# Moving every float32r operand of TensorE to a 256-byte boundary in SBUF by padding the pools

## The chip, the cores and the metric

The kernel runs on one core of one Trainium2 chip. The metric is device time in microseconds of one execution; smaller is better. The time before is the median of three runs. A separate execution was taken with the hardware profiler, and all rows below come from it.

## The reference

One layer of a hybrid encoder, applied to a prompt of 1024 tokens and a sample of 256 tokens that share all weights; model width 1024, feed-forward width 2816, four heads everywhere.

```python
def encoder_layer(x, mem, ...):
    proj = rmsnorm(x, norm_mix_w) @ w_in
    qkv_raw, ab, dn_gate, sg_u, sg_v, gate_a, gate_b = jnp.split(proj, ...)
    y_a = deltanet_branch(qkv_raw, ab, dn_gate, ...) @ w_up_a
    y_b = spatial_gating_branch(sg_u, sg_v, ...) @ w_up_b
    x = x + (sigmoid(gate_a) * y_a + sigmoid(gate_b) * y_b) @ w_out
    x = x + memory_cross_attention(rmsnorm(x, norm_xa_w), rmsnorm(mem, norm_mem_w), ...)
    gu = rmsnorm(x, norm_ffn_w) @ ffn_w_gate_up
    return x + (silu(gu[..., :D_FF]) * gu[..., D_FF:]) @ ffn_w_down
```

`deltanet_branch` is a bidirectional gated delta rule in chunks. A final RMSNorm follows. All inputs and outputs are float32.

## The kernel before

Activations lie feature-major: 128 features on the partitions, tokens along the free dimension, in the three blocks of `BLOCKS` (512, 512 and 256 tokens). Each large product is done in three TensorE products: an operand x is split into a rounded part hi, of type float32r, and the rest lo = x - hi (`split`, L124 to L126: one ScalarE copy, one subtraction on VectorE or GpSimd), and `mm3` (L110) adds hi·hi, hi·lo and lo·hi into the same PSUM bank. The built program has 6288 float32r matmuls whose moving operand is 512 columns wide, 3888 with 256 columns and 480 with 264 columns (`sgv`, L571). The rest are float32 products: the delta rule's 128-column ones, norms and transposes. A float32 matmul shows as two records in the trace.

The stages stand one behind the other: projections and spatial gating, the delta rule beside the gate projections, memory keys and values, the two up-projections, the output projection (`Seven`, L1281, products with seven instead of eight block multiplications), attention, the gate and up matrices of the feed-forward block (`ff_up`, L2082, from about 1250 us to 1895 us), and its down matrix (`down_prompt`, `down_sample`). Work beside TensorE's main stream (norms, weight splits, the delta rule) is put into the program's order by generators that a clock of TensorE's planned work wakes (`pump`, L71); once built, each engine's order is fixed.

What this case is about is where tiles lie. SBUF tiles come from pools (`pool`, L170). Pools of the default side are stacked upward from the low end of each partition, in the order in which they are opened; pools with `side="right"` are stacked downward from the high end, 229376 bytes. A tile's address so follows from the sizes of all that was opened before it. The first pool, `const` (L175), holds five tiles whose sizes do not add up to a multiple of 256 bytes; behind it follow `w` (weights: `raw`, `whi`, `wlo`), `h` (activations: `hi0`, `lo0`, `hi1` ...) and all later pools of that side. What lies between float32r tiles behind it adds up to multiples of 256 bytes, except where the table below names another offset, so one offset runs through most of the kernel. The addresses of float32r operands, modulo 256 bytes, are:

| operands | byte offset modulo 256 |
|---|---|
| `whi`, `wlo`, `hi*`, `lo*`, `xf`, `bhl`, `yb`, `mhi`, `mlo`, `yhi`, `ylo`, `kv`, `pt` and nearly all else | 96 |
| on the right side, pool `wx` of `Seven` (`ah`, `al`, `r..`), `attq` (`q0`, `q1`), `ffd` (`ahl`) | 224 |
| on the right side, pool `ffn` inside `x2`, `x0` (`t4h`, `t4l`) | 160 |
| `svh`, `svl` as moving operand: 264 columns are 1056 bytes, so the eight slices of a tile start at all multiples of 32 | 0, 32, ... 224 |

By matmul: of the 6288 with 512 columns, 5580 have both operands at 96, 456 have the stationary one at 224 and the moving one at 96, and 252 (those on `t4h`, `t4l`) have the moving one at 160 and the stationary one at 96. Of the 3888 with 256 columns, 3504 are at 96 and 96, and 384 at 96 and 224. Nowhere are both operands at a multiple of 256.

When `sg` is open (its tiles `ab`, `vg`, `wk5`, `gm` and others), the default side reaches to byte 229344: 32 bytes are free.

`decays` (L521) computes the delta rule's decays in five slices z, s_, q_, p_, r_ of the tile `wk5`, each [128, 10, 8], and writes the result into a tile `gm` of [128, 2, 40], 320 bytes (L553 to L557), from which two small TensorE products read it (L562). `s_` is last read at L549, before `gm` is written.

Of the kernel before, what the change touches and what calls it, by code (L numbers as in the profile page):

```python
# [8 lines left out]
F32 = mybir.dt.float32  # L9
# [8 lines left out]
P = 128  # L18
# [36 lines left out]
class Trunk:  # L55
# [44 lines left out]
    def mm(self, out, l, r, start=True, stop=True, more=False):  # L100
        n = 1
        for x in out.shape[1:]:
            n *= x
        if l.dtype == F32R:
            self.clock += max(n, 16) / 2.4 * (1 if n >= 256 else 4)
        else:
            self.clock += (4 * n / 2.4) if n > 1 else 2
        self.nc.tensor.matmul(out, l, r, start=start, stop=stop, skip_group_check=more)  # L108
# [10 lines left out]
    def tr(self, out, x, ident):  # L119
        self.clock += 64  # L120
        self.nc.tensor.transpose(out, x, ident)  # L121
# [42 lines left out]
def trunk_kernel(ctx: ExitStack, tc: tile.TileContext, a):  # L164
# [5 lines left out]
    def pool(name, bufs=1, **kw):  # L170
        if kw.get("space") != DRAM:
            kw["reuse_waits"] = "tile"
        return tc.tile_pool(name=name, bufs=bufs, **kw)

    cp = ctx.enter_context(pool("const"))  # L175
    wp = K.wp = ctx.enter_context(pool("w", 2))
    hp = ctx.enter_context(pool("h"))
    pm = ctx.enter_context(pool("pm", 4, space=PSUM))
# [39 lines left out]
    def bank(p=pq, tag="b"):  # L218
        return p.tile([P, 512], F32, tag=tag, name="bank")
# [195 lines left out]
    r = xp.tile([P, 512], F32, tag="nacc", name="seed", bufs=2)[:, :NS]  # L415
# [73 lines left out]
    sp = ses.enter_context(pool("sg"))  # L489
# [31 lines left out]
    def decays():  # L521
        S.activation(rows[:, 0:8], rows[:, 0:8], AF.Exp)
        wk5 = sp.tile([P, 5, NCH, 8], F32, name="wk5")
        z, s_, q_, p_, r_ = (wk5[:, i] for i in range(5))
        gm = sp.tile([P, 2, 40], F32, name="gm")

        def cols(dst, d):
            return (
                (dst[:, d, 0:32].rearrange("p (h c) -> p c h", h=4), slice(0, 8)),
                (dst[:, d, 32:40].rearrange("p (h c) -> p c h", h=4), slice(8, 10)),  # L530
            )

        S.activation(z, ab[:, :, 0:8], AF.Tanh, scale=0.5)
        for d in range(2):
            for dst, cc in cols(beta, d):
                V.tensor_scalar(out=dst, in0=z[:, cc, 4 * d : 4 * d + 4], scalar1=0.5, scalar2=0.5, op0=ALU.mult, op1=ALU.add)
        V.tensor_tensor(out=r_, in0=ab[:, :, 8:16], in1=rows[:, 8:16].unsqueeze(1).to_broadcast([P, NCH, 8]), op=ALU.add)
        V.scalar_tensor_tensor(out=z, in0=r_, scalar=-1.0, in1=r_, op0=ALU.mult, op1=ALU.max)
        S.activation(z, z, AF.Exp, scale=-1.0)
        yield 1500  # L540

        V.tensor_scalar(out=s_, in0=z, scalar1=2.0, scalar2=None, op0=ALU.add)
        V.reciprocal(s_, s_)
        V.tensor_tensor(out=s_, in0=s_, in1=z, op=ALU.mult)
        V.tensor_tensor(out=q_, in0=s_, in1=s_, op=ALU.mult)
        V.tensor_scalar(out=p_, in0=q_, scalar1=1.0 / 17, scalar2=None, op0=ALU.mult)
        for j in (15, 13, 11, 9, 7, 5, 3):
            V.scalar_tensor_tensor(out=p_, in0=p_, scalar=1.0 / j, in1=q_, op0=ALU.add, op1=ALU.mult)
        V.scalar_tensor_tensor(out=p_, in0=p_, scalar=1.0, in1=s_, op0=ALU.add, op1=ALU.mult)  # L549
        V.tensor_scalar(out=r_, in0=r_, scalar1=0.0, scalar2=None, op0=ALU.max)  # L550
        V.scalar_tensor_tensor(out=p_, in0=p_, scalar=2.0, in1=r_, op0=ALU.mult, op1=ALU.add)
        for d in range(2):
            for dst, cc in cols(gm, d):  # L553
                n = cc.stop - cc.start
                V.scalar_tensor_tensor(
                    out=dst, in0=p_[:, cc, 4 * d : 4 * d + 4], scalar=-1.0,
                    in1=rows[:, 4 * d : 4 * d + 4].unsqueeze(1).to_broadcast([P, n, 4]), op0=ALU.mult, op1=ALU.mult)  # L557
        gr = sp.tile([40, 2, P], F32, name="gr")
        yield 9000
        pr = bank()  # L560
        for d in range(2):
            mm(pr[:40, d * P : (d + 1) * P], gm[:, d, :], tri[d])  # L562
        V.tensor_copy(gr, pr[:40, : 2 * P].rearrange("p (d t) -> p d t", d=2))
        SY.dma_start(grd.rearrange("d r t -> r d t"), gr)
        yield 3000
        pt = bank()
        for d in range(2):
            tr(pt[:, d * 40 : (d + 1) * 40], gr[:, d, :], ident[:40, :40])
        V.tensor_copy(gcol.rearrange("p d r -> p (d r)"), pt[:, :80])
# [79 lines left out]
    for b in (2, 0, 1):  # L649
        K.main(sgv(b))  # L650
        if b == 2:
            bias()
        elif b == 1:
            K.side(decays())
        K.main(sgu(0, b))
        K.main(sgu(1, b))
# [430 lines left out]
    for job in plan:  # L1087
        if job[0] == "conv":
            kind, h = job[1:]
# [290 lines left out]
                evac(x, ps)  # L1380

    wxs = ExitStack()
    so = Seven(a["w_out"], wxs.enter_context(pool("wx", side="right")), mt, smp_h)

    def both_of(*phs):
# [345 lines left out]
    gsd = dp.tile([NFF, P, NS], F32, name="gsd")  # L1731
    x2s, x0s, xhs = ExitStack(), ExitStack(), ExitStack()
    x2p = x2s.enter_context(pool("x2", side="right"))
    x0p = x0s.enter_context(pool("x0", side="right"))
    xhp = xhs.enter_context(pool("xh", side="right"))

# [401 lines left out]
    x2p = ctx.enter_context(pool("x2"))  # L2138
# [336 lines left out]
```

## Time and profile before

| | |
|---|---|
| time, median of three runs | 2192.83 us (2191.4 to 2193.04) |
| span of the profiled execution | 2190.4 us, 2.4 us below that median |
| matmul records | 12436 |
| VectorE busy | 1355.2 us (62%) |
| ScalarE busy | 880.0 us (40%) |
| GpSimd busy | 571.7 us (26%) |
| DMA | 255.13 MB, mean 116 GB/s |

The span is the time from the first to the last instruction of the program; the 2.4 us are what lies around it. On TensorE the length of a record is not what a matmul costs: records overlap, since the next one starts while the last one drains. The cost of one matmul in a stream is the distance from its start to the start of the next, and the timeline view gives the starts.

### The profile page before, as it was taken

To read this page: it belongs to the slowest core of one execution; us is meant where nothing else is said; L and a number is where in the kernel's file an instruction comes from. 1 tells how busy PE (TensorE), PEld (TensorE's weight loads), DVE (VectorE), ACT (ScalarE), POOL (GpSimd) and SP (SyncE) were. 2 spreads that over 40 slices of the span, in tenths; PEclk is the share of its full clock that TensorE was granted. 3 is DMA by queue.
4 is the path that set the end of the run, shared out by engine and by line. 5 is a ranking of instruction groups with operands and counts; after the bars stand their busy time and mean duration, and the time that the engine had idled before them with its cause. 6 is when DMAs were issued, how large, how long until landed. Compare 5 with 4: busy or idle time off the path is not lost.

```text
span 2190.4 us, 32379 instructions
## 1 busy us (share of the span) xinstructions
PE 2175.7 (99%) x12436; PEld 1904.7 (87%) x12436; DVE 1355.2 (62%) x2614; ACT 880.0 (40%) x1649; POOL 571.7 (26%) x379
## 2 busy tenths in 40 slices
PE   9999999999999999999999999999999999999998
PEld 8988888898888899888988888888888888888888
DVE  7867587686874845677644556544434444378575
ACT  6533262544535553124544533332322323343454
POOL 2010000100000000042412432566666665200031
PEclk9999999999999999999999999999999999999999
DMA  5221412323234546741522421322222222493531
GB/s 194 92 93 58 120 57 88 81 66 93 75 121 122 170 137 209 238 144 42 189 68 105 165 97 63 104 83 86 82 77 80 82 97 92 139 349 122 206 111 58
DMA packets 188309, 255.13 MB, mean 116 GB/s; under 512 B 71978, under 2 KB 102266, under 8 KB 188154
## 3 DMA queue, kind: packets, MB, share of 16 engines
q1 hardware_dynamic: 170618, 228.15, 31.7%
q10 hardware_dynamic: 17536, 24.91, 3.1%
q8 instruction: 97, 1.59, 0.3%
q14 instruction: 58, 0.48, 0.1%
HBM read 179.05 MB, written 73.97 MB: 116 GB/s over the span
## 4 chain that ended last, share of the span: by engine, by line
PE 92%; DVE 5%; ACT 2%; issue 1%; DMA 1%; POOL 0%; DVEq 0%; SPq 0%; ACTq 0%; POOLq 0%
PE bank L108 91%; PE bank L121 1%; DVE acc L689 1%; DVE U L931 1%; DMA braw<-gq 1%; DVE zt L923 0%; ACT U L913 0%; PE bank L386 0%; ACT UT L910 0%; DVE nt L288 0%; DVE gb L810 0%; DVE gs L689 0%; ACT junk L511 0%; ACT acc L687 0%; DVE lo L126 0%
## 5 line engine op out<-in xcount | busy, mean ns | idle before, releaser
L108 PE MATMUL bank<-hi,whi 128*128 128x512 f32 (+1 forms) x1976 | 701.7, 355 | 0.2 <-DVE vg L487 0.2
L108 PE MATMUL bank<-hi,wlo 128*128 128x512 f32 (+1 forms) x1976 | 687.0, 348 | 0.0
L108 PE MATMUL bank<-lo,whi 128*128 128x512 f32 (+1 forms) x1976 | 686.8, 348 | 0.0
L108 PEld LDWEIGHTS bank<-hi,wlo 128*128 128x128 f32 x1976 | 373.5, 189 | 48.7
L108 PEld LDWEIGHTS bank<-hi,whi 128*128 128x128 f32 x1976 | 374.4, 189 | 44.7 <-DVE vg L487 1.0
L108 PEld LDWEIGHTS bank<-lo,whi 128*128 128x128 f32 x1976 | 374.6, 190 | 43.0
L125 ACT ACTIVATE whi<-raw 128x1024 fp32r<-128x1024 f32 (+1 forms) x136 | 136.9, 1009 | 252.9 <-PE bank L108 221.6
L126 POOL TENSOR_TENSOR wlo<-raw,whi 128x1024 fp32r<-128x1024 f32 x65 | 159.4, 2454 | 294.1 <-ACT whi L125 294.1
L108 PE MATMUL bank<-bhl,whi 128*128 128x512 f32 x408 | 125.9, 390 | 0.1
L126 DVE TENSOR_TENSOR wlo<-raw,whi 128x1024 fp32r<-128x1024 f32 (+1 forms) x71 | 80.7, 1139 | 70.4 <-ACT whi L125 70.2
L126 POOL TENSOR_TENSOR wlo<-x,whi 128x1024 fp32r<-128x1024 f32 x40 | 97.5, 2437 | 46.8 <-ACT whi L125 46.8
L2106 DVE TENSOR_TENSOR x<-x,bank 128x512 f32<-128x512 f32 x21 | 14.4, 688 | 124.3 <-ACT x L1901 124.3
L689 DVE SCALAR_TENSOR_TENSOR acc<-craw,sm,acc 128x510 f32<-128x510 f32 (+1 forms) x96 | 73.8, 769 | 27.6 <-ACT acc L687 25.9
L108 PEld LDWEIGHTS bank<-bhl,whi 128*128 128x128 f32 x408 | 76.4, 188 | 16.5 <-ACT whi L125 0.5
L1914 DVE SCALAR_TENSOR_TENSOR t<-t,x 128x512 f32<-128x512 f32 x42 | 64.4, 1532 | 28.4 <-ACT t L1913 28.4
L125 ACT ACTIVATE whi<-x 128x1024 fp32r<-128x1024 f32 (+1 forms) x48 | 49.2, 1025 | 78.1 <-PE bank L108 70.1
L108 PE MATMUL bank<-bhl,wlo 128*128 128x512 f32 x204 | 79.6, 390 | 0.5 <-DVE wlo L126 0.5
L1923 DVE SCALAR_TENSOR_TENSOR t<-bank,t 128x512 f32<-128x512 f32 (+1 forms) x44 | 24.5, 558 | 82.6 <-PE bank L108 82.6
L108 PE MATMUL bank<-bhl,ahl 128*128 128x512 f32 x312 | 75.0, 395 | 0.0
L1050 ACT ACTIVATE gs<-bank 128x512 f32<-128x512 f32 (+1 forms) x60 | 31.2, 520 | 103.1 <-PE bank L108 93.7
L1901 ACT ACTIVATE x<-bank 128x512 f32<-128x512 f32 x63 | 37.6, 597 | 82.1 <-PE bank L108 79.8
L108 PEld LDWEIGHTS bank<-bhl,ahl 128*128 128x128 f32 x312 | 58.7, 188 | 13.7
(416 smaller groups left out, 4513.8 us busy)
## 6 DMA issues: line engine op xcount, KB each, us to landing
raw<-in_w_gu SPq DMA_DIRECT2D x44, 512.0 KB, 3.3
braw<-gq SPq DMA_DIRECT2D x14, 1024.0 KB, 6.6
raw<-in_w_g SPq DMA_DIRECT2D x20, 512.0 KB, 3.3
gq<-t SPq DMA_DIRECT2D x33, 256.0 KB, 2.0
gtd<-gs ACTq DMA_DIRECT2D x32, 256.0 KB, 2.3
w<-in_w_dn SPq DMA_DIRECT2D x8, 1024.0 KB, 12.2
raw<-in_w_qkv SPq DMA_DIRECT2D x12, 512.0 KB, 3.5
gq<-r SPq DMA_DIRECT2D x22, 256.0 KB, 2.0
```

Source lines behind the costliest of these rows:

```text
L108: self.nc.tensor.matmul(out, l, r, start=start, stop=stop, skip_group_check=more)
L121: self.nc.tensor.transpose(out, x, ident)
L125: self.last_hi = self.nc.scalar.activation(hi, src, AF.Copy).ins
L126: (eng or self.nc.vector).tensor_tensor(out=lo, in0=src, in1=f32(hi), op=ALU.subtract)
L689: V.scalar_tensor_tensor(out=dst, in0=src, scalar=wj, in1=dst, op0=ALU.mult, op1=ALU.add)
L931: V.scalar_tensor_tensor(out=U[d][:, hs, :], in0=quad(pu), scalar=mine[:, 2 * level + d : 2 * level + d + 1], in1=U[d][:, hs, :], op0=ALU. ...
L1050: S.activation(t, ps, AF.Tanh, scale=0.5)
L1901: S.activation(t, ps, AF.Copy)
L1914: V.scalar_tensor_tensor(out=t, in0=t, scalar=1.0, in1=src, op0=ALU.add, op1=ALU.mult)
L1923: V.scalar_tensor_tensor(out=out, in0=u, scalar=sign, in1=t, op0=ALU.mult, op1=ALU.mult)
L2106: V.tensor_tensor(out=c22, in0=c22, in1=pe, op=ALU.add)
```

## The change

Three pads move pools: 160 bytes at the start of `const`, 224 bytes (`LINE - 32`) at the high end in a pool of their own opened ahead of `wx`, and 192 bytes at the start of the right-hand pool `x2`. To make room for the first one where the default side is full, `gm` is no longer a tile: it is a view of `s_`, whose contents are dead by then and whose 320 bytes are the same size.

```diff
+    LINE = 256
+
+    def pad(p, size):
+        p.tile([P, size // 4], F32, name="pad")
+
     cp = ctx.enter_context(pool("const"))
+    pad(cp, 160)
...
         z, s_, q_, p_, r_ = (wk5[:, i] for i in range(5))
-        gm = sp.tile([P, 2, 40], F32, name="gm")
+        gm = s_.rearrange("p c h -> p (c h)").rearrange("p (d r) -> p d r", d=2)
...
     wxs = ExitStack()
+    pad(ctx.enter_context(pool("edge", side="right")), LINE - 32)
     so = Seven(a["w_out"], wxs.enter_context(pool("wx", side="right")), mt, smp_h)
...
     x2p = x2s.enter_context(pool("x2", side="right"))
+    pad(x2p, 192)
```

With it, both operands of all 10176 float32r matmuls of 512 and 256 columns start at multiples of 256 bytes. The 480 of 264 columns have the stationary operand there; their moving slices still start at all multiples of 32. The pads are never written or read. The built program has the same instructions in the same order on every engine, with the same waits; six of them name another tile (four that write the decays and two that read them), and addresses differ. The float32 tiles of the delta rule move as well, from 64 to 224 modulo 256, and the constants from 128 to 32.

## The prediction

> **What bounds the kernel now.** I read the page from the top: how long TensorE is busy, whether its clock is held back, and which engine makes up the chain that ended last.
>
> ```profile
> span 2190.4 us, 32379 instructions
> PE 2175.7 (99%) x12436; PEld 1904.7 (87%) x12436; DVE 1355.2 (62%) x2614; ACT 880.0 (40%) x1649; POOL 571.7 (26%) x379
> PEclk9999999999999999999999999999999999999999
> PE 92%; DVE 5%; ACT 2%; issue 1%; DMA 1%; POOL 0%; DVEq 0%; SPq 0%; ACTq 0%; POOLq 0%
> ```
>
> TensorE is busy in 2175.7 of 2190.4 us, its clock is granted in full, and 92% of the chain is its own work. So the time is the number of matmuls times their spacing. Nothing is saved by shortening another engine, and a change that moves only addresses can matter in one way: by the spacing. The second reading is therefore the timeline of TensorE, for the starts. In the rows below, the columns are start, length, engine, line, operation and tiles (out<-moving,stationary).
>
> ```profile
> 1886.63 0.39 PE L108 MATMUL bank<-hi,whi 128*128 128x512 f32 x1
> ...
> 1889.36 0.39 PE L108 MATMUL bank<-whi 128*128 128x512 f32 x1
> ...
> 1892.19 0.28 PE L108 MATMUL bank<-lo,whi 128*128 128x256 f32 x1
> ...
> 1894.95 0.40 PE L108 MATMUL bank<-t4h,whi 128*128 128x512 f32 x1
> ...
> 1897.75 0.40 PE L108 MATMUL bank<-hi,whi 128*128 128x512 f32 x1
> ```
>
> From 1886.63 to 1889.36 stand 12 matmuls of 512 columns, both operands at offset 96: 2.73/12 = 0.2275 us each. From 1892.19 to 1894.95 stand 23 of 256 columns, same offsets: 2.76/23 = 0.120. From 1894.95 to 1897.75 stand 12 of 512 columns whose moving operand `t4` is at 160: 2.80/12 = 0.2333. They use weights of the same tiles in the same stage, so the offset of the moving operand is the likely difference. The stationary one shows it too:
>
> ```profile
> L108 PE MATMUL bank<-xf,whi 128*128 128x512 f32 x128 | 39.5, 389 | 0.0
> L108 PE MATMUL bank<-xf,ah 128*128 128x512 f32 x96 | 30.1, 395 | 0.0
> ```
> ```profile
> 977.56 0.62 PE L108 MATMUL bank<-xf,ah 128*128 128x512 f32 x2
> ...
> 980.34 0.64 PE L108 MATMUL bank<-xf,ah 128*128 128x512 f32 x2
> ```
>
> The moving tile `xf` is the same; with the stationary `ah` at 224 instead of `whi` at 96 a record's mean grows from 389 to 395 ns, and the 12 starts between 977.56 and 980.34 are 2.78/12 = 0.2317 us apart. So addresses do cost time here, though no row shows offset 0 on both sides. What a read costs by its address is my inference. One more row helps:
>
> ```profile
> 99.64 0.28 PE L108 MATMUL bank<-svh,hi 128*128 128x264 f32 x1
> ...
> 102.54 0.40 PE L108 MATMUL bank<-hi,whi 128*128 128x512 f32 x1
> ```
>
> These are 24 matmuls of 264 columns, whose moving slices run through all eight offsets: 2.90/24 = 0.1208 us. Eight more columns than 256 cost next to nothing. That fits a read in whole lines of 128 bytes, 32 columns: from offset 96, 512 columns touch 17 lines, 256 touch 9, and 264 touch 9 at any of the eight offsets. Per line that is 227.5/17 = 13.4, 120.0/9 = 13.3 and 120.8/9 = 13.4 ns: one price for three widths. It doesn't explain why 160 costs more than 96 (17 lines both), so it is a model, not a finding.
>
> **The change part by part.** The same instructions, waits and queues remain, so no step is moved past a queue and no wait is added. What changes is the spacing of 10176 matmuls.
>
> 512 columns at offset 0. By the line model 16 lines: 16 x 13.4 = 214 ns. By a straight line through the two moving offsets (227.5 at 96, 233.3 at 160; 0.09 ns a byte) 219 ns. Between them stands a row that reads no stream of addresses at all, the float32 products on one repeated column:
>
> ```profile
> 9.00 2.75 PE L386 MATMUL bank<-h 128*128 128x512 f32 x6
> ```
> ```profile
> 9.43 1.89 PE L386 MATMUL bank<-h 128*128 128x512 f32 x4
> ```
>
> The second view starts one record later and ends one earlier, so a record costs 2.75 - 1.89 = 0.86 over two, 0.43 us. Float32 streams at about half of float32r's pace, so half of it, 0.215, is the nearest to a stream without address cost. I take 216 ns; the ends are 214 and, if offset 0 is no better than 96, 227.5.
>
> 256 columns. By lines 8 x 13.3 = 106 ns. The nearest row for short matmuls, each with its own weight load, is the delta rule's:
>
> ```profile
> 327.67 0.61 PE L108 MATMUL bank<-st,acc 128*128 128x128 f32 x4
> ```
> ```profile
> L108 PE MATMUL bank<-st,acc 128*128 128x128 f32 x256 | 38.3, 275 | 0.0
> ```
>
> (0.61 - 0.275)/3 = 0.112 us for a float32 record of 128 columns, as long a stream as 256 of float32r. Between 106 and 112, nearer to the row, I take 110; the ends are 106 and 120. For 264 columns, 9 lines remain: nothing.
>
> The sum: 5580 x (227.5 - 216) = 64.2 us; 456 with the stationary at 224, (231.7 - 216) = 7.2; 252 on `t4`, (233.3 - 216) = 4.4; 3888 x (120 - 110) = 38.9. In all 114.7 us of TensorE's stream.
>
> Not all of it stays, since the other engines keep their pace:
>
> ```profile
> 300.00:400.00 100.00, 99.68 (x606) 87.90 (x605) 77.07 (x219) 42.08 (x114) 2.61 (x10) 1.00 0.28 81
> 900.00:1000.00 100.00, 100.00 (x508) 85.31 (x507) 84.00 (x102) 26.88 (x31) 35.60 (x12) 1.00 0.44 146
> 1500.00:1600.00 100.00, 100.00 (x531) 86.27 (x530) 42.62 (x44) 29.38 (x40) 62.69 (x33) 1.00 0.24 85
> ```
> ```profile
> PE bank L108 <- DVE vg L487: 1.1, 2, 0.9
> PE bank L108 <- DVE U L931: 1.0, 1, 1.0
> ```
>
> The columns of the windows are PE, PEld, DVE, ACT and POOL busy with their counts, then clock, DMA share and GB/s. In the feed-forward block (1500 to 1600) the busiest helper has 37% of its time free: a stream 6% shorter fits. In the first 1100 us VectorE is at 77 to 84%, and its work there is chains that answer a product before TensorE may go on (the delta rule's `U`, L931; gating, L487; the output projection's banks). TensorE waits there already, 1.1 and 1.0 us by the rows. What is late next is those answers. Half of the 114.7 us falls into these 1100 us, half of the span; I let a third of that half, 19 us, return as waits; the ends are nothing and the whole half. Net 95.7, from 2190.4 + 2.4 = 2192.8: **2097 us**.
>
> The decays' view on `s_` keeps four VectorE instructions and two products:
>
> ```profile
> L555 DVE SCALAR_TENSOR_TENSOR gm<-wk,rows x4: 159/182/208, 113.0 to 113.3; 128x32 f32<-128x32 f32 x2, 128x8 f32<-128x8 f32 x2
> ```
>
> VectorE runs in order, so the dead slice costs no wait: 0. Had the view made each twice as long, it were 4 x 0.18 = 0.7 us of VectorE, hidden behind TensorE's stream. Float32 operands shift from 64 to 224; the records on stationary tiles at many offsets share one mean (275 ns above, at 64), so 0; 3 ns more on each of this row's 256 records would be 0.8 us, to either side.
>
> The Trainium skill, "TensorE: Matmul & The Clock Gate", section "Wait — 56ns, not 53.3ns?", gives the warm spacing as columns over 2.4 GHz plus 2.5 ns: an estimate of 215.8 and 109.2 ns. The trace of before doesn't agree (227.5 and 120.0); by the rule as the floor the sum would be 119 instead of 115 us.
>
> **The rivals.**
>
> *Offsets don't matter, only that both operands share one.* All rows fit that as well: 96 with 96 is fast, 160 with 96 and 96 with 224 are slow. Then 0 with 0 costs what 96 with 96 costs, and only 708 matmuls gain: 456 x 4.2 + 252 x 5.8 = 3.4 us, so 2189 us, not told from no change. For it speaks that the 256-column ones at 96 and 224 have no longer records (284 ns for `hi,al`) than those at 96 and 96 (283); against it the single price of 13.4 ns a line.
>
> ```profile
> L108 PE MATMUL bank<-hi,al 128*128 128x256 f32 x32 | 9.1, 284 | 0.0
> L108 PE MATMUL bank<-hi,wlo 128*128 128x256 f32 x784 | 221.7, 283 | 0.0
> ```
>
> The Trainium skill, "SBUF — State Buffer", section "Specifications (TRN2)", has SBUF read in cachelines of 16 bytes. By that rule, all of 96, 160 and 224 begin a line already and the pads change nothing. The steady 233.3 against 227.5 speaks against lines as short as that.
>
> *Only wide matmuls gain.* Short ones are held at 0.120 by their weight load, which is as long at offset 0. For it: 264 columns cost what 256 cost. Then 75.8 us of the sum are left, less a sixth: 63, so 2130 us.
>
> *Slower: 96 is the good place.* If reads from the boundary on collide, as 160 does now, all 5580 go to 233.3: 5580 x 5.8 = 32 us, while nothing is won elsewhere: 2225 us. It decides as soon as the spacing of the wide ones lies over 227.5. For it: at 96 the matmuls are the fastest of all rows. Against it: no row at a smaller offset.
>
> **How the numbers follow.** My forecast has a chance of 0.5: 2097 us, and with its bounds (all kept: 2078; 214 and 106 ns, all kept: 5580 x 13.5 + 8.1 + 4.9 + 3888 x 14 = 143, so 2050; half returned: 2135) mostly 2068 to 2130. The wide-only rival has 0.2 (2130), shared offsets or 16-byte lines 0.2 (2189), slower 0.1. A range from 2068 to 2191 leaves out slower and the forecast's lowest end, two in ten. Faster by over 0.2%, about what a measurement of this kernel can tell from no change: 0.7; within: 0.2; slower: 0.1.
>
> **What would show it.** In the timeline: starts of 512-column matmuls 0.216 apart, `t4` and `xf,ah` no longer apart from the rest, 256-column ones at 0.110, 264-column ones still at 0.121. In the windows of the feed-forward block 531 matmuls in 100 us become about 560. PE's waits grow in the first 1100 us, on VectorE. I am wrong if the wide spacing stays at 0.227 (shared offsets), if the short one stays at 0.120 (weight load), or if the spacing falls and the span doesn't.

## The result, and the profile after

| | before | after |
|---|---|---|
| time, median of 20 runs each, us | 2192.64 (2191.31 to 2195.4) | 2188.43 (2186.86 to 2189.45) |
| ratio after to before, 95% interval | | 0.998 (0.9974 to 0.9987) |
| span of the profiled execution, us | 2190.4 | 2186.0 |

The change saves 4.2 us, where 95.7 were forecast. The time lies inside the forecast's wide range (2068 to 2191), but at the end that was put there for the rival with a chance of 0.2, not where the forecast's own sum stands. The page of the changed kernel looks like that of before:

```profile
span 2186.0 us, 32379 instructions
PE 2171.1 (99%) x12436; PEld 1904.5 (87%) x12436; DVE 1352.1 (62%) x2614; ACT 879.4 (40%) x1649; POOL 569.8 (26%) x379
PE 92%; DVE 5%; ACT 2%; issue 1%; POOL 0%; DMA 0%; DVEq 0%; ACTq 0%; POOLq 0%
```

TensorE is still the bound, and its busy time shrinks by 4.6 us. The timeline of TensorE after the change, at the place where the prediction read its spacings (start, length, engine, line, operation, tiles out<-moving,stationary):

```profile
1885.57 0.39 PE L108 MATMUL bank<-hi,whi 128*128 128x512 f32 x1
...
1888.29 0.39 PE L108 MATMUL bank<-whi 128*128 128x512 f32 x1
...
1891.12 0.28 PE L108 MATMUL bank<-lo,whi 128*128 128x256 f32 x1
...
1893.88 0.40 PE L108 MATMUL bank<-t4h,whi 128*128 128x512 f32 x1
...
1895.04 0.39 PE L108 MATMUL bank<-t4h,wlo 128*128 128x512 f32 x1
...
1896.63 0.39 PE L108 MATMUL bank<-hi,whi 128*128 128x512 f32 x1
...
1897.99 0.39 PE L108 MATMUL bank<-hi,whi 128*128 128x512 f32 x1
```

From 1885.57 to 1888.29 stand 12 matmuls of 512 columns, now with both operands at 0: 2.72/12 = 0.2267 us. The prediction had 0.2275 at 96, but that came from starts rounded to 0.01 us: in nanoseconds, as the trace has them, the 12 take 2720 before and 2720 after. From 1891.12 to 1893.88 stand 23 of 256 columns: 2.76/23 = 0.120, to the digit what it was. Only `t4` moved: its 12 take 1893.88 to 1896.63, 2.75/12 = 0.229 instead of 0.2333. And that is a mean of two parts. The first five, right behind the short ones, stand 1.16/5 = 0.232 apart; the last seven 1.59/7 = 0.227. A wide stream settles to its good spacing only after some matmuls. Over the whole trace, 149 wide streams follow 256-column matmuls; their first five distances have means of 233.4, 235.8, 228.6, 232.4 and 230.8 ns, the sixth 226.9, and all later ones 226.6 to 227.0. The same is seen from the other side in one more row of before:

```profile
1899.14 0.39 PE L108 MATMUL bank<-hi,whi 128*128 128x512 f32 x1
```

There the six matmuls behind `t4`, from 1897.75 on, take 1.39 us, 0.232 each, although both operands lie at 96. After the change the six from 1896.63 to 1897.99 take 1.36, 0.227.

The other place of the prediction, the stationary `ah` (timeline and groups by form, after):

```profile
974.40 0.62 PE L108 MATMUL bank<-xf,ah 128*128 128x512 f32 x2
...
977.12 0.62 PE L108 MATMUL bank<-xf,ah 128*128 128x512 f32 x2
```
```profile
L108 PE MATMUL bank<-xf,ah 128*128 128x512 f32 x96 | 29.6, 389 | 0.0
```

12 starts in 2.72 us, 0.2267 instead of 0.2317; the record's mean falls from 395 to the 389 ns that `xf,whi` always had. The 264-column matmuls stay:

```profile
99.52 0.28 PE L108 MATMUL bank<-svh,hi 128*128 128x264 f32 x1
...
102.42 0.40 PE L108 MATMUL bank<-hi,whi 128*128 128x512 f32 x1
```

24 in 2.90 us, 0.1208 as before. The windows (PE, PEld, DVE, ACT and POOL busy with counts, clock, DMA share, GB/s) show the same per stage:

```profile
900.00:1000.00 100.00, 100.00 (x512) 85.68 (x511) 82.88 (x101) 27.30 (x31) 36.09 (x12) 1.00 0.45 149
1500.00:1600.00 100.00, 100.00 (x532) 86.53 (x531) 42.46 (x44) 29.38 (x40) 62.59 (x33) 1.00 0.24 85
```

The feed-forward block does 532 matmuls in 100 us instead of 531, where some 560 were expected. The stage with `ah` does 512 instead of 508.

Put together from the distances between starts in both traces, instruction by instruction, the matmuls with `ah` or `ahl` (stationary at 224 before) give 2.2 us, those on `t4` 1.2, the wide ones at 96 and 96 another 1.7, and the rest returns a net 0.9: 4.2 in all. It helps to part the distances into plain ones (under 300 ns for 512 columns, under 160 for fewer) and longer ones, among which are TensorE's waits. The plain ones alone shrink by 4.7 us. Of the 1.7 at 96 and 96 they hold 0.7, which lies in the first seven matmuls behind an unlike one; the rest of it, like what is returned, stands in the longer distances. The 4512 wide ones that follow no unlike one within 30 cost the same in both traces to 0.03 ns, so 0 with 0 is no better than 96 with 96. The mean of the wide ones that lay at 96 and 96 is 228.0 ns before and 227.9 after; that of the short matmuls is 119.6 in both.

### The profile page after: what moved, and what is told of

The parts are those of the page before. It is cut to its first block, busy times and chain, and to the rows that moved or that the text cites. A ratio compares the mean times of both kernels' runs of the same rounds, so it can differ in the third digit from the quotient of the medians.

```text
span 2186.0 us, 32379 instructions
## 1 busy us (share of the span) xinstructions
PE 2171.1 (99%) x12436; PEld 1904.5 (87%) x12436; DVE 1352.1 (62%) x2614; ACT 879.4 (40%) x1649; POOL 569.8 (26%) x379
## 3 DMA queue, kind: packets, MB, share of 16 engines
q8 instruction: 97, 1.59, 0.3%
## 4 chain that ended last, share of the span: by engine, by line
PE 92%; DVE 5%; ACT 2%; issue 1%; POOL 0%; DMA 0%; DVEq 0%; ACTq 0%; POOLq 0%
PE bank L108 90%; PE bank L121 1%; DVE acc L695 1%; DVE U L937 1%; PE bank L392 0%; DVE zt L929 0%; ACT U L919 0%; DMA gb<-grd 0%; POOL al L1315 0%; ACT UT L916 0%; DVE nt L294 0%; DVE gb L816 0%; DVE gs L695 0%; ACT junk L517 0%; DVE nacc L259 0%
```

## The experiments

Three explanations stood after this. **A**: a moving operand at 0 is faster by itself, as the line model has it, and something else in the kernel hides that. **B**: only the difference of the two start addresses modulo 256 bytes matters, and equal is best. **C**: the 11 ns by which a wide matmul stays over the 216 I had taken have nothing to do with where an operand starts.

### A map of start addresses, TensorE alone

Eight moving tiles `ma` to `mh` and eight stationary tiles `sa` to `sh`, at offsets 0, 32 ... 224:

```python
m = [cp.tile([P, 520], F32R, tag="m" + c, name="m" + c) for c in "abcdefgh"]
s = [cp.tile([P, 136], F32R, tag="s" + c, name="s" + c) for c in "abcdefgh"]
...
for n in (512, 256):
    for j in range(8):
        for i in range(8):
            run(weights(j), wide(i, n))
```

> This kernel leaves out the whole computation; it runs TensorE alone: 16 matmuls in a row for each of 8 x 8 pairs of offsets modulo 256 (moving tiles ma to mh and stationary tiles sa to sh at 0, 32, ... 224), 512 and then 256 columns wide, then float32r products on one repeated column and bfloat16 products. Theory A (the failed one: reads in whole 128-byte lines, counted from a boundary): the row of moving offset 0 costs about 216 ns at 512 columns and about 110 at 256, all other offsets 227 and 120, whatever the stationary offset. Theory B (only the difference of the two offsets counts): 227 ns on the diagonal, whatever the offset, and 229 to 235 off it, with 233 for a moving operand 64 bytes past the stationary one. Theory C (the 11 ns over a clean stream of 216 belong to float32r itself): one repeated column as moving operand stays at 227 as well, and bfloat16 falls to 216; if they belong to the reading of the moving operand, the repeated column falls to 216 too; if to the reading of the weights, the repeated stationary column falls to 216.

The timeline of this kernel, 16 matmuls a row where the shapes are alike (the first row is the rest of a longer run of one pair):

```profile
14.67 12.18 PE L53 MATMUL bank<-ma,sa 128*128 128x512 f32 x53
26.68 3.90 PE L53 MATMUL bank<-mb,sa 128*128 128x512 f32 x16
...
219.94 3.89 PE L53 MATMUL bank<-mf,sg 128*128 128x512 f32 x16
223.66 3.79 PE L53 MATMUL bank<-mg,sg 128*128 128x512 f32 x16
227.29 3.90 PE L53 MATMUL bank<-mh,sg 128*128 128x512 f32 x16
...
358.98 1.98 PE L53 MATMUL bank<-me,sg 128*128 128x256 f32 x16
360.79 2.05 PE L53 MATMUL bank<-mf,sg 128*128 128x256 f32 x16
362.68 2.08 PE L53 MATMUL bank<-mg,sg 128*128 128x256 f32 x16
364.59 2.05 PE L53 MATMUL bank<-mh,sg 128*128 128x256 f32 x16
```

With the stationary tile at 192 (`sg`), a wide moving tile at 192 (`mg`) costs (227.29 - 223.66)/16 = 0.2269 us, one at 160 (`mf`) 0.2325. That is the diagonal of the map. Taken from the trace without each row's first two distances, at every offset from 32 to 224 equal addresses cost 226.6 to 227.5 ns; a moving operand 64 bytes past the stationary one costs 229.1, and every other pair 232.5 to 234.5. Offset 0 with 0 is no better than 96 with 96: `ma,sa` costs (26.68 - 14.67)/53 = 0.2266. For 256 columns it is the other way round: equal costs 1.91/16 = 0.119 (`mg,sg`), and 192 past the stationary one only 1.81/16 = 0.113 (`me,sg`); over the map equal is 119.6, most others are 117 to 119, and seven of the eight pairs 192 past lie at 113.4 to 115.0.

A fell here. Of B, the part that equal starts are best held for wide matmuls. For C, the last rows of the same timeline repeat one column as moving operand (`ma,sa`), then one column as stationary operand (`mb,sa`):

```profile
381.55 3.66 PE L53 MATMUL bank<-ma,sa 128*128 128x512 f32 x16
385.05 3.87 PE L53 MATMUL bank<-mb,sa 128*128 128x512 f32 x16
388.75 1.95 PE L53 MATMUL bank<-ma,sa 128*128 128x256 f32 x16
```

A wide matmul whose moving operand walks through no addresses costs 3.50/16 = 0.219 us; one whose weights walk through none 3.70/16 = 0.231, no better than an unlike pair. So most of the 11 ns go when the moving operand stands still. By where it starts they do not go: no pair in the map is under 226.6, and C holds so far.

### All operands at 96

The changed kernel without the pad of `const` and without the view in `s_`, the right side moved to 96 as well:

```diff
-    pad(cp, 160)
...
-        gm = s_.rearrange("p c h -> p (c h)").rearrange("p (d r) -> p d r", d=2)
+        gm = sp.tile([P, 2, 40], F32, name="gm")
...
-    pad(ctx.enter_context(pool("edge", side="right")), LINE - 32)
+    pad(ctx.enter_context(pool("edge", side="right")), 128)
```

> All float32r operands at 96 modulo 256 instead of 0: no pad in const, gm a tile of its own again, the right-hand pads 128 and 192 bytes. Theory B (only the difference of the two operands' offsets counts): the same as the change, 2188.4 us, spacing 227 everywhere, t4 and ah like the rest. Rival (the 256-byte boundary itself counts for something): between the change and before, up to 2192.6 us.

Measured: 2189.02 us (2187.68 to 2189.35), ratio to the kernel before 0.9981 (0.9973 to 0.999), where the change has 0.998 (0.9974 to 0.9987). In the two traces the plain distances of all wide matmuls differ by 0.1 us together. So the boundary of 256 bytes is worth nothing that these runs can tell, and neither the 160 bytes of `const` nor the shared room of `gm` is needed.

### Only the left side at 0

The changed kernel without its two pads on the right side, so that `t4` and `ah` stay unlike the rest:

```diff
-    pad(ctx.enter_context(pool("edge", side="right")), LINE - 32)
...
-    pad(x2p, 192)
```

> The change without its two right-hand pads: all of the default side at 0, ah and ahl stay at 224, t4 at 160. Theory B: nothing is gained, since the 708 matmuls still have unlike offsets (differences 32 and 160, by the map 233.0 and 234.4 ns), so 2193 us. Rival (boundary): 5580 matmuls with both operands on it, so most of the gain stays, 2188 to 2190 us.

Measured: 2191.44 us, ratio 0.9996 (0.9987 to 1.0004), no gain. Here 5580 wide and 3504 short matmuls have both operands at 0. The timeline at `ah`:

```profile
974.60 0.63 PE L108 MATMUL bank<-xf,ah 128*128 128x512 f32 x2
...
977.40 0.63 PE L108 MATMUL bank<-xf,ah 128*128 128x512 f32 x2
```

12 starts in 2.80 us, 0.233: the moving operand lies at 0 here, and is slow with the stationary one at 224, where the change has 0.2267 with both at 0. The whole gain of the change comes from the two right-hand pads.

### Most operands unlike

The price, many times over: the changed kernel with the pool `h` (`hi`, `lo`), and with it the later pools of its side, moved to 160, while the weights of pool `w` stay at 0. That sets the starts of 5148 wide and 2304 short matmuls 160 apart.

```diff
     hp = ctx.enter_context(pool("h"))
+    pad(hp, 160)
```

> The change with 160 more bytes ahead of the pool h, so that activations lie at 160 and the weights of pool w at 0. 5148 of the 512-column matmuls then have a difference of 160 (234.4 ns in the map instead of 227), 252 one of 96; 2304 of the 256-column ones go from 119.6 to 117.4. Theory B: 5148 x 7.4 + 252 x 6.1 - 2304 x 2.2 - 384 x 0.4 = 34 us more stream than the change, so about 2222 us. Rival (boundary counts): each moving operand off it costs what the failed line model says, at most as before, 2193 us.

Measured: 2215.05 us (2214.32 to 2215.85), 26.6 more than the change; ratio to before 1.0102 (1.0088 to 1.0115). Timeline and groups by form:

```profile
1906.43 0.40 PE L108 MATMUL bank<-hi,whi 128*128 128x512 f32 x1
...
1908.54 0.39 PE L108 MATMUL bank<-hi,whi 128*128 128x512 f32 x1
```
```profile
L108 PE MATMUL bank<-lo,whi 128*128 128x256 f32 x784 | 220.7, 281 | 0.0
```

9 wide matmuls in 2.11 us: 0.234. Matmul by matmul against the trace of the change, in plain distances: 5000 of the wide pairs 160 apart cost 6.2 ns more each, 31.0 us; the 252 on `t4` (now 96 apart, at 232.5 ns) 0.9 us; the wide ones left equal 0.4; and 2252 short pairs 160 apart 1.7 ns less each, 3.8 us, at 117.9. Together 28.5 us, of which 26.6 are seen. So the difference alone moves the time by a per cent. A short matmul's record shrinks from 283 to 281 ns at the same time, as the map says it must.

### Narrow moving operands at 192

The map says that wide streams want equal offsets and short ones unlike ones. This kernel gives the 256-token tiles a pool of their own, 192 bytes past the weights modulo 256, and all else stays at 0; the bytes used are those of the change.

```diff
-    pad(cp, 160)
+    narrow = ctx.enter_context(pool("narrow"))
+    narrow.tile([P, 96 // 4], F32, tag="low", name="pad")
...
+            return (narrow if tag in ("hi2", "lo2") else self.p).tile(shape, dt, tag=tag, **kw)
...
-    hp = ctx.enter_context(pool("h"))
+    hp = Split(ctx.enter_context(pool("h")))
...
+    narrow.tile([P, 64 // 4], F32, tag="high", name="pad")
```

> The change with the tiles of 256 tokens (tags hi2 and lo2) in a pool of their own ahead of w, at 192 modulo 256, all else at 0; no byte more is used. 2784 of the 256-column matmuls then have a difference of 192, where the map has 113.9 ns instead of 119.6. Theory B with the map: 2784 x 5.7 = 15.9 us less stream than the change, 2173 us if other engines keep up. Rival (the map's repeated operands don't carry over to streams whose operands alternate): no change, 2188 us.

Measured: 2180.4 us (2179.91 to 2182.96), ratio to before 0.9946 (0.9933 to 0.996). It beats both kernels: the one before by 11.6 us, the changed one (timed in another set of runs) by 8.0. The timeline, and the groups by form:

```profile
1882.49 0.28 PE L108 MATMUL bank<-hi,whi 128*128 128x256 f32 x1
...
1885.31 0.39 PE L108 MATMUL bank<-t4h,whi 128*128 128x512 f32 x1
...
1888.03 0.39 PE L108 MATMUL bank<-hi,whi 128*128 128x512 f32 x1
```
```profile
L108 PE MATMUL bank<-lo,whi 128*128 128x256 f32 x784 | 219.8, 280 | 0.0
```

24 short matmuls in 2.82 us: 0.1175 instead of 0.120. The 12 wide ones on `t4` behind them are at once at 2.72/12 = 0.2267: behind these short ones no settling is seen. So it is over the 116 such places of the trace: the first three distances have a mean of 227.4 ns each, all later ones 226.6 to 227.2. The mean over 2736 distances of the moved short ones is 117.2 ns, 2.4 less than at equal offsets: 6.6 us. The wide ones, which now need not settle, save another 3.0 us in plain distances, 0.5 ns each. With 0.3 us lost elsewhere that is 9.3, more than the 7.4 by which the span falls (2186.0 to 2178.6); the rest is idle time of TensorE between its records, 7.8 us here and 5.9 in the change. My expectation had the map's 113.9, and got less than half of that gain; with `hi` and `lo` both 192 past their weights, the kernel doesn't do what the map's repeated pair did.

### The kernel's own pattern, TensorE alone

Why 117.2 and not 113.9? In the map one operand is repeated 16 times; the kernel alternates hi and lo. So, with the weights `wh` and `wl` at 0 and hi and lo at each of the eight offsets:

```python
T.matmul(ps, wh[:, w], h[:, x], start=k == 0, stop=False)
T.matmul(ps, wh[:, w], l[:, x], start=False, stop=False)
T.matmul(ps, wl[:, w], h[:, x], start=False, stop=k == ks - 1)
```

> Leaves out the whole computation; TensorE alone, in the kernel's own pattern: hi with weights hi, lo with weights hi, hi with weights lo, eight weight slices in a row, the weights at 0, hi (ha to hh) and lo (la to lh) each at all eight offsets modulo 256, 512 and then 256 columns. Theory B (the difference of each matmul's two operands decides): 512 columns are fastest, 227 ns, with both at 0 and about 233 elsewhere; 256 columns are at 119.6 with both at 0 and least, by the kernel with 192 about 117.2, with both near 192 or 32. Rival (what counts is the distance between one matmul's operands and the next one's): pairs in which hi and lo lie at unlike offsets come out unlike the mean of their two matmuls, some under 117.

Measured (settled means of 18 matmuls): in the wide pattern hi and lo both at 0 give 226.7 ns, and every other pair 228.7 to 234.4, also where only one of the three products is unlike (lo at 32: 231.5). In the short pattern 0 and 0 give 120.0 and nearly all others 117.1 to 120.0; 192 and 192, the arrangement of the experiment above, gives 117.8, and the lowest two of the 63 measured are 116.4. So the 113.9 doesn't carry over to the kernel's pattern, and no arrangement tried here would beat that kernel by much. Nor do the map's prices for unlike wide pairs carry over. With hi at 128 and lo at 0, two of the three products have starts 128 apart, which cost 233.3 each in the map:

```profile
201.60 0.39 PE L55 MATMUL bank<-he,wh 128*128 128x512 f32 x1
...
205.95 0.39 PE L56 MATMUL bank<-la,wh 128*128 128x512 f32 x1
```

These 19 take 4.35 us, 0.2289 each, where the mean of the map's prices would be 231.1. With lo at 32 only one product is unlike, and it is 231.5 where that mean would be 229. So equal starts throughout are best for wide matmuls, but what an unlike one costs depends on its neighbours too: theory B's "only the difference" is too simple, and the rival in the expectation is right in that part.

### Widths, bfloat16, and one side standing still

```python
for n in (128, 192, 256, 320, 384, 448, 512):
    for i in (0, 2, 3, 6):
        run(weights(0), wide(i, n), 24)
for n in (512, 256):
    for i in range(8):
        run(sbf, mbf[i][:, :n], 24)
```

> TensorE alone; the whole computation is left out. 24 matmuls each, weights loaded anew for every one. (1) float32r moving operands at offsets 0, 64, 96 and 192 past the same weights at 0, with 128, 192, 256, 320, 384, 448 and 512 columns: where between 256 columns (equal offsets slowest, 119.6 against 114 to 118) and 512 (equal offsets fastest, 227 against 229 to 234) the sign changes. Theory P (how far the weight load of the next matmul has come when the stream of this one ends decides, so each unlike offset shifts a matmul by a fixed amount): the differences from the equal case are +6 ns or 0 from some width on, and don't grow with it. Theory Q (each column read at an unlike offset costs a little): the loss grows in proportion, 6 x (columns - 300)/200 or so: about 2.5 ns at 384, 4 at 448, 6 at 512. (2) bfloat16 moving operands at all eight offsets past one bfloat16 weight tile: if the conflict belongs to SBUF's addresses as such, unlike offsets cost several ns here too; if it belongs to the float32r stream, all eight give 215.8 (512) and 109.2 (256). (3) weights that are one column repeated, at the offset of the moving operand and at another: if only the start of the weights mattered, equal starts would give 227 and unlike ones 233; if the weight load must walk through addresses in step with the stream, both give 231 as in the first map. Moving operands that are one column repeated: 218.7 whatever the weights' offset.

The timeline, 24 matmuls a row; `ma`, `mc`, `md`, `mg` lie at 0, 64, 96 and 192, `sa` at 0, and `nb` and `nc` are bfloat16 at 32 and 64:

```profile
25.20 2.84 PE L54 MATMUL bank<-mc,sa 128*128 128x128 f32 x24
27.88 2.84 PE L54 MATMUL bank<-md,sa 128*128 128x128 f32 x24
...
52.58 2.99 PE L54 MATMUL bank<-mg,sa 128*128 128x256 f32 x24
55.41 3.68 PE L54 MATMUL bank<-ma,sa 128*128 128x320 f32 x24
58.93 3.68 PE L54 MATMUL bank<-mc,sa 128*128 128x320 f32 x24
62.45 3.69 PE L54 MATMUL bank<-md,sa 128*128 128x320 f32 x24
65.97 3.68 PE L54 MATMUL bank<-mg,sa 128*128 128x320 f32 x24
69.49 4.32 PE L54 MATMUL bank<-ma,sa 128*128 128x384 f32 x24
...
116.67 5.77 PE L54 MATMUL bank<-md,sa 128*128 128x512 f32 x24
122.28 5.76 PE L54 MATMUL bank<-mg,sa 128*128 128x512 f32 x24
127.88 5.35 PE L54 MATMUL bank<-na,sbf 128*128 128x512 bf16 x24
133.07 5.34 PE L54 MATMUL bank<-nb,sbf 128*128 128x512 bf16 x24
138.25 5.34 PE L54 MATMUL bank<-nc,sbf 128*128 128x512 bf16 x24
```

A matmul's cost is the distance from the start of a row to that of the next, over 24; the settled means are from the trace, without a row's first four distances. 128 columns cost 2.68/24 = 0.112 us, and 192 columns the same 0.112 at all four offsets, so there the columns don't set the pace. 256 columns 192 past their weights (`mg,sa`) cost 2.83/24 = 0.118 us here, where the map had 113.8 ns for the same pair: even a repeated short pair has more than one steady spacing. 320 columns cost 3.52/24 = 0.147 at every offset. At 384 the settled means are 173.3, 173.3, 176.7 and 174.7 ns, at 448 they are 202.5, 200.1, 205.2 and 202.0, at 512 228.0 (227 for the last ones), 228.7, 233.7 and 233.4. The loss against equal starts is neither a fixed amount (theory P) nor proportional to the columns (theory Q): nothing at 320, and at 448 an operand 64 past the weights is even faster than an equal one. Both fell. What the run does settle is the operand type and the two sides. In bfloat16 all eight offsets cost 5.18/24 = 0.2158 us, 256 columns 0.1092. In float32r, weights that are one repeated column give 231.3 to 231.8 ns, whether their address equals the moving one's or not; a repeated column as moving operand gives 218.7 to 219.1, whatever the weights' offset.

## Why the prediction was wrong, step by step

**The bound was right.** TensorE's spacing sets the time: its plain distances shrink by 4.7 us in the change, grow by 28.5 with most operands unlike and shrink by 9.3 with the narrow ones at 192, where the times move by -4.2, +26.6 and -8.0. What is between stands in the longer distances, and part of that is chance: between the change and the kernel at 96 the plain distances agree to 0.2 us, while TensorE's idle time between records is 5.9 us in one trace and 7.1 in the other.

**The reading that addresses cost time was right, and so were the rows.** Equal starts are fast, 160 with 96 and 96 with 224 slower: the experiments have the same. Not every size is the same, though. `t4`, 64 bytes past its weights, settles at 233.3 ns in the kernel before, where the map has 229.1 for that difference and the kernel's pattern alone 228.9.

**The step that failed is "512 columns at offset 0. By the line model 16 lines", with its "I take 216 ns", and the same step for 256 columns, "I take 110".** The model counted lines from a boundary, for the moving operand alone. At 0 the runs have 226.7 and 119.6 to 120. What counts for wide matmuls is whether the moving and the stationary start are equal modulo 256 bytes, and they were already for 5580 wide and 3504 short ones. So the terms 64.2 and 38.9 us of the sum were both nothing. (The 227.5 itself came from rounded starts; it was 226.7.) The price of 13.4 ns a line, alike for 256, 264 and 512 columns, was what had convinced me, and was a coincidence of these widths: 192 columns cost no more than 128, and 320 columns from a boundary, 10 lines, cost 14.7 ns a line. The row that should have stopped it was in the text: 160 costs more than 96 at the same count of lines. 103 of the 115 us stood on offset 0 being fast by itself, which no row had shown.

**The terms of 456 and 252 matmuls were right in kind.** With 227.5 in place of 216 as the goal they are the rival "offsets don't matter, only that both operands share one": 1.9 + 1.5 = 3.4 us, 2189 us. Measured were 2.2 + 1.2 at these matmuls, 0.9 at wide ones up to seven places behind them, which no term had, and longer distances that nearly cancel: 2188.4. Its argument, too, was the sound one: of the records that I quoted it left none unexplained.

**The floor of 0.215 us from the float32 row** was near what a repeated column gives in float32r, 218.7. But a stream that walks through no addresses is no goal for one that must, and moving its start doesn't bring it there.

**"A third of that half, 19 us, return as waits"** was not put to the test by a change that takes 4 us. (Of the 114.7 us, 50 fall into the first 1100 us by the counts, not quite half.) The largest saving here, 9.3 us of spacing with the narrow operands at 192, shows as 7.4 in the span, but about 1 us of such a difference can be chance, as above. The two rows of waits on `U` and `vg` together went from 2.1 to 3.0, a change no larger than that:

```profile
PE bank L108 <- DVE U L937: 1.9, 2, 1.0
PE bank L108 <- DVE vg L493: 1.1, 2, 0.9
```

**"Only wide matmuls gain"** fell with the step above. Its reason, that short ones are held at 0.120 by their weight load, isn't borne out either: matmuls with a weight load each run at 0.112 with 192 columns and with 128, and short ones went to 0.1175 in the kernel when they were moved to 192. **"96 is the good place"** fell with the kernel that has all at 96: the same time. Its price of 5.8 ns for a wide unlike matmul was near; the experiment with `h` at 160 paid 6.2.

**What the two pages of the Trainium skill gave.** "TensorE: Matmul & The Clock Gate", section "Wait — 56ns, not 53.3ns?", has the spacing as columns over 2.4 GHz plus 2.5 ns. In bfloat16 the last run agrees to the digit, 215.8 and 109.2 ns at every offset; float32r stays at 227 and 120, so for this kernel's operands it was no floor to reach for. "SBUF — State Buffer", section "Specifications (TRN2)", has SBUF read in cachelines of 16 bytes, by which pads of 32-byte steps should do nothing. For the boundary itself that is what the runs show (all at 96 as good as all at 0), but it doesn't give the 6 ns between equal and unlike starts.

**What stays open.** The loss goes when the moving operand stands still, but not when the weights do, and 227 is only reached when both walk from equal starts. It is not there in bfloat16, nor at 320 columns. One guess is that the next weight load and the running stream read the same memory at once and get in each other's way (PEld is busy 87% of the span beside PE's 99%). No row shows such a conflict. The weight loads' records are no longer for unlike starts than for equal ones; in bfloat16 they are half as long (groups by form, of the map and of the last run):

```profile
L53 PEld LDWEIGHTS bank<-mc,sc 128*128 128x128 f32 x32 | 5.0, 189 | 0.7
L53 PEld LDWEIGHTS bank<-mc,sa 128*128 128x128 f32 x32 | 5.0, 188 | 0.7
```
```profile
L54 PEld LDWEIGHTS <-sbf 128*128 128x128 bf16 x384 | 37.5, 98 | 25.1 <-issue 0.3
```

Nor do these runs tell a matmul's own weights from those of the next one: in nearly all streams here the two lie at the same offset. Why a pair 64 apart costs 233 ns in one stream and 229 in another, and the mixed numbers at 384 and 448 columns, follow from no rule that I have.

## What to carry to other kernels

Before a change of layout is priced, ask which quantity the rows of the profile vary: here they varied the difference of two addresses as much as the address itself, and the cheaper reading (only unlike pairs gain) explained every row. In float32r, let 512-column moving operands start at the same address as their weights modulo 256 bytes, and 256-column ones at another (192 gained 2.4 ns in this kernel, 160 gained 1.7); where the common offset lies is not worth a byte. A model that fits three rows and fails a fourth has no claim to the whole sum.

## What the runs showed of the hardware that was not expected

- float32r, weights loaded anew for each matmul: with one pair repeated, 512 columns cost 227 ns at equal offsets and 229 to 234.5 at others; 256 columns 119.6 at equal and 113.4 to 119.9 at others. In the kernel's own pattern 512 columns cost 226.7 with both at 0 and 228.7 to 234.4 otherwise, 256 columns 116.4 to 120.0.
- bfloat16 in the same loop: 215.8 and 109.2 ns, the same at all eight offsets of the moving operand.
- At 128 and at 192 columns such a float32r matmul costs 111.7 ns alike.
- The spacing has a memory: behind short matmuls at equal offsets (149 places after the change) the first five wide ones cost 229 to 236 ns before they settle at 227; behind unlike wide ones (36 places before it) the first seven cost 228 to 235; behind short ones at 192 (116 places) the first cost 227.4 already.
